# A decoder layer on one core: the second half of the input rows read in 32x32 blocks and turned on VectorE, the sample probabilities turned one step later

## The chip, the cores and the metric

The kernel runs on one core of a Trainium2 chip. A core has TensorE (PE, matrix products out of SBUF into PSUM), VectorE (DVE), ScalarE (ACT), GpSimd (POOL), and queues from which the engines and SyncE (SP) issue DMA transfers. The metric is the device time of one execution in microseconds (us), lower is better: 977.61 us before the change (median of 3 runs, 977.39 to 978.35).

## The reference

One layer of a hybrid decoder, over a prompt of 512 tokens and 32 sample tokens (8 sequences of 4), model width 1024, in float32. Cut to what matters here:

```python
h = x * rsqrt(mean(x * x, axis=-1) + EPS) * g          # RMSNorm of the rows
xr, q, k, v, g = split(h @ w_in)                       # one combined input projection, 4608 columns in 128-wide chunks
m = (sigmoid(g_A) * (lru(conv(xr)) @ w_lru_o) + sigmoid(g_B) * (attention(q, k, v) @ w_attn_o)) @ w_out
x = x + RMSNorm(m)
x = x + RMSNorm((gelu(gate) * val) @ w_down)           # gate, val: conv(RMSNorm(x) @ w_up)
```

The attention of the prompt looks back over 128 keys; that of the sample tokens over a cache of 128 keys and the new ones. Besides the rows, the kernel gives back the states of the recurrence, of the convolutions and the key and value caches.

## The kernel before

The activations lie turned: a tile holds 128 channels on its partitions and the 544 tokens along its columns, in two halves a = 0 (tokens 0 to 255) and a = 1 (tokens 256 to 543: 256 of the prompt and the 32 of the sample group). Every float32 operand of a product is split into a high and a low part, and three products stand for one: high by high, low by high, high by low.

**The input.** The rows of x arrive with tokens on the partitions (`xload`, L377), 128 tokens by 512 channels in each transfer. TensorE turns them through an identity matrix into PSUM: the first half in `turn_a` (L468), 16 transposes, and the second in `turn_b` (L523), 24 transposes: for each of 8 channel tiles k two blocks of 128 tokens and the 32 sample tokens. `hsplit` (L452) multiplies the turned tile by the norm's gain and splits it: ACT writes the high part hH[k], DVE the low part hL[k] = x*g - hH. The root of each row's mean square (`xsquare` for the sums, `roots` for the rest) is applied later, to the results of the projection: `roots` makes a diagonal tile dg on DVE, and a product ones by dg on TensorE (`ps_rep`) spreads it over the partitions as `rep`. The turned rows themselves are needed again for the residual some 320 us later: `keep_a` and `keep_b` copy them from PSUM into tiles xn, `put_away` (L515) sends these to DRAM from POOL's queue, and `x_again` (L1130) reads them back from SP's queue, 8 transfers.

**The projection.** `step` (L344) multiplies one 128-wide chunk of w_in by one half of h: 8 tiles by 3 products, 24 matmuls, into one of 3 PSUM buffers of the pool psm. After the matmuls `tick` runs what the other engines have to do at that place: the generators whose time has come (`sides`: a table of step numbers, `start_at`, says which of them starts at which step), the results of the step before (`late`), the splitting of the next weight chunk (`wsplit_hi` on ACT, L283, and `wsplit_lo` on DVE, L290), and the list `last`. So the order of the instructions on PE, ACT, DVE and POOL is that in which this code writes them, and each engine works its list off in order; SP's list follows from the same program.

The chunks come in the order 16, 18, 8, 9, 10, 11, 17, ... (16 and 17 are keys, 18 and 19 values, the others queries). The first `FIRST = 5` are multiplied by half 0 while half 1 is still being turned, then the same 5 by half 1, and from there every chunk by both halves. In the half-0 steps (`mmhalf_low_last`, L323) the products with the low weights come last; in the half-1 steps (`mmhalf`, L335) each tile k has its three products at once, so that hL[k] is needed right after hH[k]. `norms` (L560) is the generator around the change: it issues `keep_a`, the two calls of `turn_b`, the sums of squares of the rows 256 and up, and `roots(2, 5)`.

**Weights.** `wload` (L251) reads a chunk of 512 KB from SP's queue into one of 5 buffers raw. Chunks 16, 18, 8, 9 and 10 are asked for at the head of the program, chunk 11 as the sixth, after the many small loads of gains, biases and tables. Chunk 11 is split after the second half-1 step.

**Sample attention.** `sample_attn` (L873) runs twice (g = 0, 1) as a generator with a step of the projection between its parts: the probabilities are made by `softmax_b`, then turned on TensorE (`pst`, L909 to L911), copied, multiplied by the values (`pso`), and turned back (`psot`, L928).

Of the kernel before, what the change touches and what calls it, by code (L numbers as in the profile page):

```python
# [11 lines left out]
F32 = mybir.dt.float32  # L12
# [5 lines left out]
P = 128  # L18
# [26 lines left out]
T_BUFS = 10  # L45
RAW_BUFS = 5
SLOT = 568
CH = 4
CHAIN = 10
# [27 lines left out]
FILL = 1  # L77
TURNED = 8
GATES = (51, 53, 55, 57, 72, 73, 74, 75)
# [44 lines left out]
def hawk_step(ctx, tc, I, O):  # L124
# [21 lines left out]
    def T(name, dt=F32):  # L146
        return tp.tile([P, FLAT + 4], dt, tag="t", name=name)

# [99 lines left out]
    def wname(i):  # L248
        return "_".join(str(z) for z in order[i])

    def wload(i):  # L251
        key = order[i]
        raw = wraw[i] = rp.tile([P, KD, P], F32, tag="raw", name="raw_" + wname(i))
        if key[0] == "wg":
            for z, nme in enumerate(("lru_wr", "lru_wi")):
                nc.sync.dma_start(out=raw[:, 4 * z:4 * z + 4, :],
                                  in_=I[nme][0, 4 * key[1]:4 * key[1] + 4].rearrange("n c d -> c n d"))
        else:
            nc.sync.dma_start(out=raw, in_=wsrc(key))
# [11 lines left out]
    def wsplit_hi(un, eng=None):  # L271
        i, u = un // 2, un % 2
        hl = []
        for x in "hl":
            if order[i] in in_slots:
                t_ = S(f"w{x}{u}_{wname(i)}", F32R)[:, 0:512]
                t_ = t_.rearrange("p (k n) -> p k n", k=4)
            else:
                t_ = wp.tile([P, 4, P], F32R, tag="w", name=f"w{x}{u}_{wname(i)}")
            hl.append(t_)  # L280
        raw = wraw[i][:, 4 * u:4 * u + 4, :]
        if eng is None:
            act.activation(hl[0], raw, AF.Copy)  # L283
        else:
            eng.tensor_copy(hl[0], raw)
        wunits[un] = hl
        return raw, hl
# [86 lines left out]
    act.activation(warm, epst, AF.Sqrt)  # L374
    xt = {}

# [74 lines left out]

    def hsplit(k, a, ps):  # L452
        g = pv[:, G_PRE + k:G_PRE + k + 1]
        act.activation(h.get(k, a, 0), ps, AF.Copy, scale=g)
        stt(h.get(k, a, 1), ps, g, f32(h.get(k, a, 0)), ALU.mult, ALU.subtract)

# [46 lines left out]

    xn = [S(f"xn{k}") for k in range(KD)]
    xdram = drp.tile([KD, P, NT], F32, name="xdram")

    tb = []

    def keep_a(k):
        act.copy(xn[k][:, 0:256], turned_a(k))  # L510

    def keep_b(k, ps):
        (dve.tensor_copy if k % 4 > 1 else act.copy)(xn[k][:, 256:NT], ps[:, :288])

    def put_away():  # L515
        for k in range(KD):
            pool.dma_start(out=xdram[k], in_=xn[k][:, 0:NT])
            yield
# [3 lines left out]

    def turn_b(ks):  # L523
        tb.extend(PX(f"ps_tb{k}") for k in ks)
        for group in ((2, 3), (4,)):
            for k in ks:
                for i in group:
                    t0, n, _ = TOK[i]
                    pe.transpose(tb[k][:, t0 - 256:t0 - 256 + n], xtile(i, k), ident[:n, :n])
# [30 lines left out]
    def norms():  # L560
        xsquare(0, 1, True)
        yield from roots(0, 2)
        yield
        last.extend(lambda k=k: keep_a(k) for k in (0, 4, 1, 5, 2, 6))
        last.append(lambda: xsquares(2))
        yield
        turn_b(range(4))
        last.extend(lambda k=k: keep_a(k) for k in (3, 7))
        yield
        turn_b(range(4, KD))  # L570
        last.extend(lambda i=i: xsquares(i) for i in (3, 4))
        yield
        yield from roots(2, 5)
        dve.tensor_scalar(rq, ss[:, 1, 0:4], SCALE, None, ALU.mult)
# [302 lines left out]
    def sample_attn(g):  # L877
# [28 lines left out]
        softmax_b(s3, 1, *se)  # L906
        yield
        px = PX(f"pst{g}")
# [141 lines left out]
    start_at(1, norms())  # L1050
    start_at(13, put_away())
    start_at(1, attn_tables())
# [3 lines left out]
    for hp in range(4):  # L1056
        start_at((3, 5, 11, 18)[hp], once(load_rep, hp))
        start_at((4, 8, 15, 24)[hp], once(load_btab, hp))
    start_at(12, sample_tables())
# [22 lines left out]
    for z, c in enumerate(qkv_order[:FIRST]):  # L1082
        step(("in", c), h, 1, in_done(c), target=2 * FIRST + (0, 2, 4, 6, 6)[z])
    for c in qkv_order[FIRST:]:
# [45 lines left out]
    def x_again():  # L1130
        for k in range(KD):
            nc.sync.dma_start(out=x1[k][:, 0:NT], in_=xdram[k])
        yield
# [874 lines left out]
```

## Time and profile before

| what | value |
|---|---|
| runs before | 977.39, 977.61, 978.35 us |
| profiled execution | 977.74 us, of which the span of the profile is 976.0 us |
| PE busy | 967.6 us, 99% of the span |
| DVE, ACT, POOL busy | 758.6, 551.0, 168.8 us |
| DMA | 143.07 MB, 147 GB/s |

A row of the timeline gives the start in us from the span's start, the duration, the engine, the line, the operation, what is written and read, how many alike were put together (x4), and in brackets the idle time of the engine before it and what ended that. Instructions of one engine overlap a little, so that the step from one start to the next is shorter than a duration. SPq is the issue of a DMA from SP's queue. The clock granted to TensorE was 0.998 in this execution.

### The profile page before, as it was taken

To read this page: it belongs to the slowest core of one execution; us is meant where nothing else is said; L and a number is where in the kernel's file an instruction comes from. 1 tells how busy PE (TensorE), PEld (TensorE's weight loads), DVE (VectorE), ACT (ScalarE), POOL (GpSimd) and SP (SyncE) were. 2 spreads that over 40 slices of the span, in tenths; PEclk is the share of its full clock that TensorE was granted. 3 is DMA by queue.
4 is the path that set the end of the run, shared out by engine and by line. 5 is a ranking of instruction groups with operands and counts; after the bars stand their busy time and mean duration, and the time that the engine had idled before them with its cause. 6 is when DMAs were issued, how large, how long until landed. Compare 5 with 4: busy or idle time off the path is not lost.

```text
span 976.0 us, 20122 instructions
## 1 busy us (share of the span) xinstructions
PE 967.6 (99%) x7668; PEld 959.9 (98%) x7668; DVE 758.6 (78%) x1632; ACT 551.0 (56%) x1344; POOL 168.8 (17%) x288
## 2 busy tenths in 40 slices
PE   9999999999999999999999999999999999999997
PEld 8999999999999999999999999999999999999996
DVE  5777888857858555699967888787888888888875
ACT  6544443467476435556767665655555555556652
POOL 2152000003306331230011111101011101011024
PEclk9999999999999999999999999999999999999999
DMA  7875535632334547136157585858586766768612
GB/s 217 237 239 163 151 88 147 161 93 87 109 113 126 175 121 189 45 122 184 39 114 189 126 191 129 184 137 177 140 179 157 169 156 160 166 140 221 201 30 92
DMA packets 234204, 143.07 MB, mean 147 GB/s; under 512 B 25012, under 2 KB 218940, under 8 KB 234076
## 3 DMA queue, kind: packets, MB, share of 16 engines
q1 hardware_dynamic: 224300, 120.21, 43.9%
q0 software_dynamic: 9696, 19.42, 11.9%
q10 hardware_dynamic: 112, 2.17, 0.6%
q8 instruction: 60, 0.98, 0.4%
q14 instruction: 36, 0.29, 0.1%
HBM read 115.59 MB, written 15.17 MB: 134 GB/s over the span
## 4 chain that ended last, share of the span: by engine, by line
PE 97%; DVE 1%; ACT 1%; DMA 0%; issue 0%; SPq 0%; POOL 0%; ACTq 0%; POOLq 0%
PE pmin L165 20%; PE pmdn L165 19%; PE pux L1536 16%; PE puy L1536 8%; PE pq L1536 7%; PE pmout L165 5%; PE pmlo L165 5%; PE pmao L165 5%; PE puz L1536 4%; PE pg L165 1%; PE pvp L165 1%; PE psc L165 1%; PE ptok L165 1%; DMA pt<-pd 0%; PE ps_warm L165 0%; PE pm_first L165 0%
## 5 line engine op out<-in xcount | busy, mean ns | idle before, releaser
L165 PE MATMUL pmin<-hH,wh_in 128*128 128x256 f32 (+1 forms) x568 | 164.0, 291 | 0.0
L165 PE MATMUL pmin<-hL,wh_in 128*128 128x256 f32 (+1 forms) x568 | 162.5, 288 | 0.0
L165 PE MATMUL pmin<-hH,wl_in 128*128 128x256 f32 (+1 forms) x568 | 159.3, 288 | 0.0
L165 PE MATMUL pmdn<-fH,wh_dn 128*128 128x256 f32 (+1 forms) x448 | 129.3, 289 | 0.0
L165 PE MATMUL pmdn<-fH,wl_dn 128*128 128x256 f32 (+1 forms) x448 | 129.2, 288 | 0.0
L165 PE MATMUL pmdn<-fL,wh_dn 128*128 128x256 f32 (+1 forms) x448 | 129.0, 288 | 0.0
L165 PEld LDWEIGHTS pmin<-hH,wh_in 128*128 128x128 f32 x568 | 107.3, 189 | 1.2 <-issue 1.0
L165 PEld LDWEIGHTS pmin<-hL,wh_in 128*128 128x128 f32 x568 | 107.4, 189 | 0.1
L165 PEld LDWEIGHTS pmin<-hH,wl_in 128*128 128x128 f32 x568 | 104.8, 188 | 0.2 <-issue 0.2
L177 DVE SCALAR_TENSOR_TENSOR uc<-u,fv,uc 128x560 f32<-128x560 f32 x128 | 102.0, 797 | 1.7 <-ACT uc L1567 1.1
L165 PEld LDWEIGHTS pmdn<-fL,wh_dn 128*128 128x128 f32 x448 | 84.4, 188 | 0.0
L165 PEld LDWEIGHTS pmdn<-fH,wl_dn 128*128 128x128 f32 x448 | 84.4, 188 | 0.0
L165 PEld LDWEIGHTS pmdn<-fH,wh_dn 128*128 128x128 f32 x448 | 84.4, 188 | 0.0
L1664 ACT COPY u<-pux 128x272 f32<-128x272 f32 x52 | 20.1, 386 | 84.4 <-PE pux L1536 84.2
L168 DVE TENSOR_TENSOR u<-puy,u 128x240 f32<-128x240 f32 (+2 forms) x78 | 24.6, 343 | 48.8 <-PE puy L1536 32.2
L174 DVE TENSOR_TENSOR ft<-ft,pmdn 128x256 f32<-128x256 f32 (+1 forms) x104 | 45.0, 434 | 15.7 <-PE pmdn L165 15.7
L283 ACT ACTIVATE wh_in<-raw_in 128x512 fp32r<-128x512 f32 x70 | 42.2, 625 | 20.7 <-issue 11.0
L290 DVE TENSOR_TENSOR wl_in<-raw_in,wh_in 128x512 fp32r<-128x512 f32 x70 | 47.8, 694 | 1.0 <-ACT wh_in L283 1.0
L1567 ACT ACTIVATE uc<-u,fv 128x560 f32<-128x560 f32 x64 | 48.2, 755 | 0.0
L779 ACT ACTIVATE s<-s,st 128x256 f32<-128x256 f32 (+1 forms) x32 | 15.2, 475 | 53.8 <-DVE st L776 46.1
L168 DVE TENSOR_TENSOR wl_dn<-raw_dn,wh_dn 128x512 fp32r<-128x512 f32 x56 | 38.3, 685 | 3.8 <-ACT wh_dn L1485 3.8
L1474 POOL DMA_DIRECT2D raw_up_s<-raw_up_s x26 | 22.4, 861 | 95.8 <-DMA raw_up_s<-raw_up__11277 5.4
(761 smaller groups left out, 3388.5 us busy)
## 6 DMA issues: line engine op xcount, KB each, us to landing
raw_in<-in_w_in_dram SPq DMA_DIRECT2D x35, 512.0 KB
raw_dn<-in_w_down_dram SPq DMA_DIRECT2D x56, 256.0 KB
raw_up_s<-in_w_up_dram SPq DMA_DIRECT2D x25, 512.0 KB
raw_up_s<-raw_up_s POOLq DMA_DIRECT2D x26, 256.0 KB, 5.3
raw_ao<-in_w_attn_o_dram SPq DMA_DIRECT2D x8, 512.0 KB
raw_lo<-in_w_lru_o_dram SPq DMA_DIRECT2D x8, 512.0 KB
raw_out<-in_w_out_dram SPq DMA_DIRECT2D x8, 512.0 KB
pd<-pb SPq DMA_DIRECT2D x12, 256.0 KB
```

Of the source, the lines that this page charges most:

```text
L165: pe.matmul(out, l, r, start=start, stop=stop)
L168: dve.tensor_tensor(out=out, in0=a, in1=b, op=ALU.subtract)
L174: dve.tensor_tensor(out=out, in0=a, in1=b, op=ALU.add)
L177: dve.scalar_tensor_tensor(out=out, in0=a, scalar=s_, in1=b, op0=op0, op1=op1)
L283: act.activation(hl[0], raw, AF.Copy)
L290: (eng or dve).tensor_tensor(out=hl[1], in0=raw, in1=f32(hl[0]), op=ALU.subtract)
L779: act.activation(s3[:, j, :], s3[:, j, :], AF.Exp, bias=ng[:, j:j + 1], accum_out=sm[:, j:j + 1])
L1474: pool.dma_start(out=w["p4"], in_=w["p2"], accum_op=ALU.add)
L1536: pe.matmul(ps[:, :HN], w, x, start=start and k == 0 and i == 0, stop=stop and k == 3 and i == 2, skip_group_check=True)
L1567: act.activation(yt[j][:, 0:FLATU], u[:, 0:FLATU], AF.Copy, scale=fv[:, j:j + 1])
L1664: act.copy(e[nm_], z)
```

## The change

The rows 256 to 511 and the 32 sample rows are now read a second time, by SP, in pieces of 32 channels (128 bytes): `xblocks(yp)` fills one of four tiles xl with 4 transfers of 32 partitions by 16 pieces each, `xblocks_sample` a fifth. In these tiles each 32x32 block lies where VectorE's transpose, which turns 32x32 blocks in place, leaves the 128 channels of a tile on its partitions. `turn_b(yp)` is now 4 VectorE transposes of 128x128 elements, called four times, and `turn_sample` 4 of 128x64; they write into four tiles xb, each of two channel tiles k. The destination of the four calls interleaves the tokens: one transpose writes every eighth column. The rows are still loaded as before for the sums of squares, but later. `hsplit` of half 1 reads xb in two pieces, 256 prompt columns and 32 sample columns, on ACT and on DVE. The 8 copies `keep_b` go, since xb is already in SBUF; `keep_a` copies whole banks, 4 of 512 columns in place of 8 of 256. `put_away` sends xb and xn as 4 and 4 transfers, `x_again` reads them back as 24 transfers in place of 8.

Around it: `FIRST` goes from 5 to 6, so chunk 11 also has its half-0 step early; its weights are loaded among the first, into slots of their own (`RAWS`). Some starts of side work move by a step or more. In `sample_attn` a `yield 2` puts the transposes `pst` one step later.

```diff
-FIRST = 5
+FIRST = 6
-TURNED = 8
+TURNED = 9
...
     def wload(i):
         key = order[i]
+        if i == RAWS:
+            wraw[i] = [S(f"raw{u}_{wname(i)}")[:, 0:512].rearrange("p (k n) -> p k n", k=4) for u in range(2)]
+            for u in range(2):
+                nc.sync.dma_start(out=wraw[i][u], in_=wsrc(key)[:, 4 * u:4 * u + 4, :])
+            return
...
+    def xblocks(yp):
+        xl[yp] = S(f"xl{yp}")
+        src = xp[2 * P:4 * P, :].rearrange("(t w y) (k b f) -> b w t (y k) f", w=4, y=2, k=KD, b=4)
+        for b in range(4):
+            nc.sync.dma_start(out=xl[yp][32 * b:32 * b + 32, 0:512].rearrange("p (x f) -> p x f", f=32), in_=src[b, yp])
...
     wload(3)
+    xblocks(0)
+    xblocks(1)
+    wload(4)
+    xblocks_sample()
+    wload(5)
+    xblocks(2)
+    xblocks(3)
     for i in (2, 3, 4):
         xload(i)
-    wload(4)
...
-    def hsplit(k, a, ps):
+    def hsplit(k, a, src, z=0):
         g = pv[:, G_PRE + k:G_PRE + k + 1]
-        act.activation(h.get(k, a, 0), ps, AF.Copy, scale=g)
-        stt(h.get(k, a, 1), ps, g, f32(h.get(k, a, 0)), ALU.mult, ALU.subtract)
+        hi, lo = (h.get(k, a, j) for j in range(2))
+        spans = [((256 * z, 256 * z + 256), (0, 256)), ((512 + 32 * z, 544 + 32 * z), (256, 288))] if a else [((0, 256), (0, 256))]
+        for (i0, i1), (o0, o1) in spans:
+            act.activation(hi[:, o0:o1], src[:, i0:i1], AF.Copy, scale=g)
+        for (i0, i1), (o0, o1) in spans:
+            stt(lo[:, o0:o1], src[:, i0:i1], g, f32(hi[:, o0:o1]), ALU.mult, ALU.subtract)
...
-    def keep_a(k):
-        act.copy(xn[k][:, 0:256], turned_a(k))
-
-    def keep_b(k, ps):
-        (dve.tensor_copy if k % 4 > 1 else act.copy)(xn[k][:, 256:NT], ps[:, :288])
+    def keep_a(z):
+        act.copy(xn[z][:, 0:512], ps_ta[z])
...
-    def turn_b(ks):
-        tb.extend(PX(f"ps_tb{k}") for k in ks)
-        for group in ((2, 3), (4,)):
-            for k in ks:
-                for i in group:
-                    t0, n, _ = TOK[i]
-                    pe.transpose(tb[k][:, t0 - 256:t0 - 256 + n], xtile(i, k), ident[:n, :n])
-        for k in ks:
-            last.append(lambda k=k, ps=tb[k]: hsplit(k, 1, ps[:, :288]))
-        last.extend(lambda k=k, ps=tb[k]: keep_b(k, ps) for k in ks)
+    def turn_b(yp):
+        for kp in range(4):
+            if not yp:
+                xb[kp] = T(f"xb{kp}")
+            o = xb[kp][:, 0:512].rearrange("p (k t w y) -> p w y k t", k=2, w=4, y=2)[:, yp]
+            dve.transpose(o, xl[yp][:, 0:512].rearrange("p (y w k t) -> p w y k t", y=2, w=4, k=2)[:, kp])
+
+    def turn_sample():
+        for kp in range(4):
+            dve.transpose(xb[kp][:, 512:576], xl[4][:, 64 * kp:64 * kp + 64])
...
-        last.extend(lambda k=k: keep_a(k) for k in (0, 4, 1, 5, 2, 6))
-        last.append(lambda: xsquares(2))
-        yield
-        turn_b(range(4))
-        last.extend(lambda k=k: keep_a(k) for k in (3, 7))
-        yield
-        turn_b(range(4, KD))
-        last.extend(lambda i=i: xsquares(i) for i in (3, 4))
+        last.extend(lambda z=z: keep_a(z) for z in range(4))
+        yield
+        last.extend(lambda yp=yp: turn_b(yp) for yp in range(2))
+        yield
+        last.extend(lambda yp=yp: turn_b(yp) for yp in range(2, 4))
+        last.append(turn_sample)
+        last.extend(lambda k=k: split_b(k) for k in range(KD))
+        yield
+        last.extend(lambda i=i: xsquares(i) for i in (2, 3, 4))
...
         softmax_b(s3, 1, *se)
-        yield
+        yield 2
...
         for k in range(KD):
-            nc.sync.dma_start(out=x1[k][:, 0:NT], in_=xdram[k])
+            nc.sync.dma_start(out=x1[k][:, 0:256], in_=xdram[k % 4][:, k // 4 * 256:k // 4 * 256 + 256])
+            for lo, hi, z in ((256, SEQ, 256 * (k % 2)), (SEQ, NT, 512 + NS * (k % 2))):
+                nc.sync.dma_start(out=x1[k][:, lo:hi], in_=xdramb[k // 2][:, z:z + hi - lo])
```

On VectorE the change shows first between the half-0 steps and the first half-1 step. Before, there stand the split of chunk 10 (wl: low weights), the low part of query head 0 (qL), the first four low parts of half 1, and two of the copies that go (xn):

```order
L290 TENSOR_TENSOR wl0_in_10_449<-raw_in_10_136,wh0_in_10_448 128x512
L290 TENSOR_TENSOR wl1_in_10_452<-raw_in_10_136,wh1_in_10_451 128x512
L168 TENSOR_TENSOR qL0_475<-pmin_8_0_361,qH0_474 128x256
L177 SCALAR_TENSOR_TENSOR hL0_154<-ps_tb0_454,pv_141,hH0_153 128x288
L177 SCALAR_TENSOR_TENSOR hL1_156<-ps_tb1_455,pv_141,hH1_155 128x288
L177 SCALAR_TENSOR_TENSOR hL2_158<-ps_tb2_456,pv_141,hH2_157 128x288
L177 SCALAR_TENSOR_TENSOR hL3_160<-ps_tb3_457,pv_141,hH3_159 128x288
L513 COPY xn2_250<-ps_tb2_456 128x288
L513 COPY xn3_251<-ps_tb3_457 128x288
L168 TENSOR_TENSOR qL1_535<-pmin_9_0_421,qH1_534 128x256
```

Now, one step further on, behind the low part of query head 1, stand the second eight of the sixteen transposes, the four of the sample rows, and only behind all of them the low parts, in two pieces each:

```order
L170 TENSOR_TENSOR qL1_526<-pmin_9_0_438,qH1_525 128x256
L556 STREAM_TRANSPOSE xb0_477<-xl2_145 128x2x64
L556 STREAM_TRANSPOSE xb1_479<-xl2_145 128x2x64
...
L556 STREAM_TRANSPOSE xb0_477<-xl3_150 128x2x64
L556 STREAM_TRANSPOSE xb1_479<-xl3_150 128x2x64
...
L560 STREAM_TRANSPOSE xb0_477<-xl4_136 128x64
L560 STREAM_TRANSPOSE xb1_479<-xl4_136 128x64
...
L179 SCALAR_TENSOR_TENSOR hL0_183<-xb0_477,pv_170,hH0_182 128x256
L179 SCALAR_TENSOR_TENSOR hL0_183<-xb0_477,pv_170,hH0_182 128x32
L179 SCALAR_TENSOR_TENSOR hL1_185<-xb0_477,pv_170,hH1_184 128x256
```

What moved: the low parts of half 1, which stood in two groups behind two steps, stand in one group of 16 instructions behind 20 transposes.

On SP's queue, from the load of chunk 9 on, there stood the rows 256 and up (x2, x3) with the sample rows (x4), the weights of chunk 10, and then the small loads:

```order
L259 DMA raw_in_9_122<-in_w_in_dram 128x8x128
L381 DMA x2_0_124<-in_x_prompt_dram 128x512
L381 DMA x2_1_126<-in_x_prompt_dram 128x512
L381 DMA x3_0_128<-in_x_prompt_dram 128x512
L381 DMA x3_1_130<-in_x_prompt_dram 128x512
L381 DMA x4_0_132<-in_x_sample_dram 32x512
L381 DMA x4_1_134<-in_x_sample_dram 32x512
L259 DMA raw_in_10_136<-in_w_in_dram 128x8x128
L401 DMA rows_a_97<-in_norm_mix_post_dram 8x128
```

Now the pieces xl stand ahead of them, four transfers to a row, with chunks 10 and 11 between:

```order
L266 DMA raw_in_9_122<-in_w_in_dram 128x8x128
L388 DMA xl0_124<-in_x_prompt_dram 32x16x32 x4
L388 DMA xl1_129<-in_x_prompt_dram 32x16x32 x4
L266 DMA raw_in_10_134<-in_w_in_dram 128x8x128
L394 DMA xl4_136<-in_x_sample_dram 32x8x32 x4
L258 DMA raw0_in_11_141<-in_w_in_dram 128x4x128
L258 DMA raw1_in_11_142<-in_w_in_dram 128x4x128
L388 DMA xl2_145<-in_x_prompt_dram 32x16x32 x4
L388 DMA xl3_150<-in_x_prompt_dram 32x16x32 x4
L400 DMA x2_0_155<-in_x_prompt_dram 128x512
```

What moved: 22 more transfers stand ahead of the small loads, and so ahead of the next weight chunk behind these, which was chunk 11 and is now chunk 17.

More of the change, by code (lines that the diff above doesn't have):

```diff
@@ L46 @@
 RAW_BUFS = 5
+RAWS = 5
 SLOT = 568
+TSLOT = 576
 CH = 4
@@ L280, in wsplit_hi @@
             hl.append(t_)
-        raw = wraw[i][:, 4 * u:4 * u + 4, :]
+        raw = wraw[i][u] if i == RAWS else wraw[i][:, 4 * u:4 * u + 4, :]
         if eng is None:
@@ L374, in hawk_step, with xblocks_sample @@
     act.activation(warm, epst, AF.Sqrt)
-    xt = {}
+    xt, xl = {}, {}
+    def xblocks(yp):
[3 more added lines that the diff above has]
+            nc.sync.dma_start(out=xl[yp][32 * b:32 * b + 32, 0:512].rearrange("p (x f) -> p x f", f=32), in_=src[b, yp])
+    def xblocks_sample():
+        xl[4] = S("xl4")
+        src = xs.rearrange("t (k b f) -> b t k f", b=4, f=32)
+        for b in range(4):
+            nc.sync.dma_start(out=xl[4][32 * b:32 * b + 32, 0:256].rearrange("p (k f) -> p k f", f=32), in_=src[b])
     def xload(i, halves=(0, 1)):
@@ L502, in hawk_step @@
     xsquare(1, 1, False)
-    xn = [S(f"xn{k}") for k in range(KD)]
-    xdram = drp.tile([KD, P, NT], F32, name="xdram")
-    tb = []
-    def keep_a(k):
-        act.copy(xn[k][:, 0:256], turned_a(k))
-    def keep_b(k, ps):
-        (dve.tensor_copy if k % 4 > 1 else act.copy)(xn[k][:, 256:NT], ps[:, :288])
-    def put_away():
-        for k in range(KD):
-            pool.dma_start(out=xdram[k], in_=xn[k][:, 0:NT])
+    xn, xb = [S(f"xn{z}") for z in range(4)], {}
+    xdram = drp.tile([4, P, 512], F32, name="xdram")
+    xdramb = drp.tile([4, P, 576], F32, name="xdramb")
+    def keep_a(z):
+        act.copy(xn[z][:, 0:512], ps_ta[z])
+    def put_away():
+        for kp in range(4):
+            pool.dma_start(out=xdramb[kp], in_=xb[kp])
+        yield 4
+        for z in range(4):
+            pool.dma_start(out=xdram[z], in_=xn[z][:, 0:512])
             yield
@@ L1082, in hawk_step @@
     for z, c in enumerate(qkv_order[:FIRST]):
-        step(("in", c), h, 1, in_done(c), target=2 * FIRST + (0, 2, 4, 6, 6)[z])
+        step(("in", c), h, 1, in_done(c), target=2 * FIRST + (0, 2, 4, 6, 6, 6)[z])
     for c in qkv_order[FIRST:]:
```

11 lines of the change are left out of this document (7 added, 4 removed).

## Prediction

> **What bounds the kernel now.** I read the page first (busy time, the chain that ended last), then the waits of TensorE (PE), then the timeline of each engine over the stretch of the change, 19 to 42 us. From the page, the span, the busy times and the chain:
>
> ```profile
> span 976.0 us, 20122 instructions
> ...
> PE 967.6 (99%) x7668; PEld 959.9 (98%) x7668; DVE 758.6 (78%) x1632; ACT 551.0 (56%) x1344; POOL 168.8 (17%) x288
> ...
> PE 97%; DVE 1%; ACT 1%; DMA 0%; issue 0%; SPq 0%; POOL 0%; ACTq 0%; POOLq 0%
> ```
>
> PE is busy in 99% of the span and carries 97% of the chain. So work taken off PE shortens the time one for one, as long as no new wait comes in its place, and each us for which PE waits longer is a us more. The waits of PE hold one that the change is aimed at (columns: us, times, longest):
>
> ```profile
> PE pst L909 <- DVE ss L787: 0.7, 1, 0.7
> ```
>
> The timeline of PE around the change (start, duration; only the rows used are kept):
>
> ```profile
> 12.17 0.28 PE L165 MATMUL pmin<-hH,wh_in 128*128 128x256 f32 x1
> ...
> 15.03 0.28 PE L165 MATMUL pmin<-hH,wh_in 128*128 128x256 f32 x1
> ...
> 18.84 0.37 PE L165 MATMUL pmin<-hH,wh_in 128*128 128x256 f32 x1
> ...
> 21.78 1.40 PE L529 MATMUL ps_tb<-ident,x 128*128 128x128 f32 x12
> ...
> 23.11 0.38 PE L165 MATMUL pmin<-hH,wh_in 128*128 128x256 f32 x1
> ...
> 26.04 1.40 PE L529 MATMUL ps_tb<-ident,x 128*128 128x128 f32 x12
> ...
> 30.68 0.29 PE L165 MATMUL pmin<-hH,wh_in 128*128 128x288 f32 x1
> ...
> 33.97 0.72 PE L165 MATMUL ps_rep<-dg,ones 128*128 128x288 f32 x2
> 34.31 0.51 PE L165 MATMUL pmin<-hH,wh_in 128*128 128x288 f32 x1
> ...
> 37.72 0.22 PE L165 MATMUL psc<-kH,qH 128*128 128x128 f32 x1
> ...
> 38.34 0.35 PE L165 MATMUL pmin<-hH,wh_in 128*128 128x288 f32 x1
> ```
>
> Steps follow one another with no gap: a half-0 step from 12.17 to 15.03, the two groups of transposes at 21.78 and 26.04, half-1 steps up to 33.97, where `ps_rep` needs the diagonal tiles dg of the roots. PE does not wait there today, but VectorE (DVE) finishes just in time, as its rows below show.
>
> **The change part by part.** *Taken off PE.* A group of 12 transposes takes 23.11 − 21.78 = 1.33 us. The steps beside them are a little longer than a plain one: 23.11 to 26.04 is 2.93 and 18.84 to 21.78 is 2.94 against 2.86, so .08 for each break. Two groups give 2 × (1.33 + .08) = 2.82 us. `pst` moved a step later ends its wait, 0.67 us (0.7 in the row; it is put behind a whole step, many times that). Moving `pso` and `psot` along with it costs nothing, since later steps of the projection still lie between them and the projection that uses the result. Gain without new waits: 2.82 + .67 = 3.49 us.
>
> *The new DVE list.* The sixth half-0 step (chunk 11) only changes places with a later one: PE's total of steps is the same. So the old list's `ps_rep`, put behind one more half-0 step, would start at 33.97 + 2.86 = 36.83. That is the mark against which the new time of `ps_rep` counts; from there both lists go on alike. DVE's rows before, from the split of chunk 10 to the first use of `rep`, and two of its block transposes from the attention (stretch 47 to 54 us):
>
> ```profile
> 22.40 1.29 DVE L290 TENSOR_TENSOR wl_in<-raw_in,wh_in 128x512 fp32r<-128x512 f32 x2 [1.02 <-ACT wh_in L283]
> 23.61 0.42 DVE L168 TENSOR_TENSOR qL<-pmin,qH 128x256 fp32r<-128x256 f32 x1
> 23.94 1.78 DVE L177 SCALAR_TENSOR_TENSOR hL<-ps_tb,pv,hH 128x288 fp32r<-128x288 f32 x4
> 25.64 0.81 DVE L513 COPY xn<-ps_tb 128x288 f32<-128x288 f32 x2
> ...
> 30.26 0.68 DVE L437 SCALAR_TENSOR_TENSOR jk<-x 128x512 f32<-128x512 f32 x1
> ...
> 30.87 0.68 DVE L437 SCALAR_TENSOR_TENSOR jk<-x 32x512 f32<-32x512 f32 x1
> ...
> 31.48 0.41 DVE L168 TENSOR_TENSOR qL<-pmin,qH 128x256 fp32r<-128x256 f32 x1
> 31.82 0.14 DVE L174 TENSOR_TENSOR ss<-ss 128x3 f32<-128x3 f32 x1
> ...
> 33.73 0.17 DVE L574 TENSOR_SCALAR rq<-ss 128x4 f32<-128x4 f32 x1
> ...
> 35.16 0.46 DVE L171 TENSOR_TENSOR ks<-pmin,rep 128x288 f32<-128x288 f32 x1 [1.27 <-ACT rep L553]
> ```
>
> ```profile
> 47.55 0.43 DVE L821 STREAM_TRANSPOSE pb<-s 128x256 f32<-128x256 f32 x1
> 47.91 0.71 DVE L177 SCALAR_TENSOR_TENSOR s<-psc,rq,btab 128x512 f32<-128x512 f32 x1
> ...
> 53.41 0.70 DVE L821 STREAM_TRANSPOSE pb<-s 128x512 f32<-128x512 f32 x1
> 54.03 0.71 DVE L177 SCALAR_TENSOR_TENSOR s<-psc,rq,btab 128x512 f32<-128x512 f32 x1
> ```
>
> Prices, always from start to next start. A transpose takes .36 us for 256 columns and .62 for 512, so .26 for each 256 more; drawn down, .36 − .13 = .23 for 128 and .165 for 64. The four hL take (25.64 − 23.94)/4 = .425 for 288 columns; by the same slope .39 for 256 and .165 for 32, together .555 in place of .425. A jk is .61, a qL .33 (23.61 to 23.94), a wl pair 1.21 (22.40 to 23.61), and the chain of the roots from ss to rq 33.73 − 31.82 = 1.91. No row shows a transpose that writes every eighth column, nor one of 128 or 64 columns; .23 is the drawn-down price at the plain rate. The bounds are .13 (the columns alone) and .36 (the 256-column row, which a write at half rate would also give); I take .23, since the slope of two rows leads to it. An hL out of SBUF in place of PSUM may be shorter: the jk row, SBUF to SBUF, drawn down gives .61 − .27 = .34 for 256, so 8 × .05 = .4 us less at most; I stay with the same operation's row.
>
> ACT sets when DVE starts:
>
> ```profile
> 19.50 1.73 ACT L510 COPY xn<-ps_ta 128x256 f32<-128x256 f32 x6
> 21.69 1.19 ACT L283 ACTIVATE wh_in<-raw_in 128x512 fp32r<-128x512 f32 x2
> 22.73 0.42 ACT L708 ACTIVATE qH<-pmin 128x256 fp32r<-128x256 f32 x1
> 23.03 1.70 ACT L454 ACTIVATE hH<-ps_tb,pv 128x288 fp32r<-128x288 f32 x4
> ```
>
> In place of six copies of 256 columns and an unfinished rest stand four of 512 at the pace of the wh pair, (22.73 − 21.69)/2 = .52: 19.50 + 2.08 = 21.58, against 21.69. So chunk 10 is split as before, and DVE's first qL starts at 21.58 + (23.61 − 21.69) = 23.50. From there DVE is never without work:
>
> - qL .33, then eight transposes 8 × .23 = 1.84: 25.67
> - wl of chunk 11, 1.21: 26.88; qL .33: 27.21
> - eight transposes 1.84: 29.05; four for the sample 4 × .165 = .66: 29.71
> - sixteen hL pieces 8 × .555 = 4.44: 34.15 (ACT needs less for the high parts: 1.70/4 = .43 for 288 in one piece, and it starts earlier)
> - qL .33, three jk 3 × .61 = 1.83, qL .33: 36.64
> - roots to rq 1.91: 38.55; `ps_rep` follows rq by 33.97 − 33.73 = .24: **38.79**
>
> The mark was 36.83, so `ps_rep` starts 1.96 us later. PE's own work does not hide this: PE waits some .4 us for the split of chunk 10, then about 3 us spread over the first half-1 step for the hL, and about 1 us for dg. The waits eat the 2.82 us and 1.96 more. The hiding cover of before was that the low parts of half 1 came in two groups of four, each behind a step of PE.
>
> *Queues.* SP, ACT's waits for the next chunk, and the read-back some 300 us later:
>
> ```profile
> 27.43 16.09 SPq L259 DMA_DIRECT2D raw_in<-in_w_in_dram  x8
> ```
>
> ```profile
> 32.56 1.15 ACT L283 ACTIVATE wh_in<-raw_in 128x512 fp32r<-128x512 f32 x2 [0.21 <-DMA raw_in<-in_w_in_dram]
> ...
> 34.73 0.40 ACT L553 COPY rep<-ps_rep 128x288 f32<-128x288 f32 x1 [1.01 <-PE ps_rep L165]
> ```
>
> ```profile
> 325.38 4.63 SPq L1132 DMA_DIRECT2D x<-xdram  x8
> ```
>
> ```profile
> L283 ACT ACTIVATE wh_out<-raw_out x16: 615/622/632, 355.4 to 385.2; 128x512 fp32r<-128x512 f32 x16
> ```
>
> Chunk 11, issued at 27.43 before, was waited for until 32.56: 5.13 us at most. Chunk 17 now stands in that place, behind 22 transfers more. At the pace of the read-back, 4.63/8 = .58 each, this is at most 12.8 us later, an issue at 40.2 and a landing at 45.4; at least it is no later, with a landing by 32.6, if the gaps that the queue's small loads leave today take them all up. I estimate an issue at 36.9, nearer the upper end because chunk 11 was already waited for today, and so a landing at 42.0. ACT then splits it (22.73 − 21.69 = 1.04), copies rep (35.16 − 34.73 = .43), and DVE frees the first PSUM buffer with ks (.46): 43.9. PE asks for that buffer behind ps_rep, the products of psc and one step: 38.79 + .34 + (38.34 − 37.72) + (37.72 − 34.31) = 43.2, with a small group of transposes (.3) at 43.5. By these numbers PE waits .4 us, by the bounds of the landing 0 to 3.8; as the roots may hold PE up anyway by as much, I take .2. The 16 more read-backs at .58 take 9.3 us, to about 339; the weights behind them are first split at 355.4, so this is hidden, and uncovered it would be 9.3 us.
>
> *Sum.* +1.96 (ps_rep) − .67 (pst) + .2 (chunk 17) = +1.5 us. The profiled execution took 977.74 us, its span 976.0; that is .13 above the median of the three runs. 977.61 + 1.5 = **979.1 us**.
>
> **The rivals.** *A, the strided write is slow (slower).* Each of the sixteen transposes writes columns 32 bytes apart. If that costs as much again as the columns (.13), DVE ends 16 × .13 = 2.1 us later, and PE with it: 979.1 + 2.1 = 981.2. It decides from .26 us for a transpose, where .47 us on sixteen brings the total past 979.57, the 0.2% bound. For it: the destination is the only one of its kind here. Against it: the source and number of elements are plain. [...]
>
> *B, DVE is quicker than drawn (faster).* If the small pieces cost .1 in place of .165, the transposes .15 and the hL .34, DVE ends 12 × .065 + 16 × .08 + 8 × .05 = 2.5 us earlier, at 36.3, and PE is back in front: it gains most of the 3.49, some 974.1 to 976.5. For it: instructions that overlap on DVE. Against it: all prices already are start to start.
>
> *C, the queue decides.* If chunk 17 lands 2 us later still, at 44, its .2 becomes 2.2: 981.1; from a landing of 42.3 or so the total passes 979.57. For it: 22 transfers, many of 128-byte pieces, go ahead of it. Against it: the small loads behind idle the queue today.
>
> **How the numbers follow.** Measurement tells about 0.2% from no change, 2 us: faster is under 975.65, slower over 979.57. The forecast has .52 (own range 977.6 to 980.0, .10 of it over 979.57), A .26, C .07, B .15. Faster is B, .15; slower is A, C and the .10, .43; the rest, .42, is the same. The range of 975.5 to 982.0 takes in A and C with the bounds of the transposes, and the upper end of B; about 2 in 10 is left out.
>
> **What would show it.** In the profile after: no ps_tb rows; no wait of pst; the xb transposes at .23 us from start to start (over .26: A; under .16: B); the last hL at about 34, ps_rep at about 38.8 (36.8 or earlier: B); a wait of PE for hL of some 3 us in all and one for dg of about 1; ACT's wait for raw 17 ending near 42 (44: C). It is wrong if PE's waits between 22 and 44 us add up to less than 2.5 us or more than 6.5.

## The result, and the profile after

The changed kernel takes 987.93 us (median of 5 runs, 986.69 to 989.44) where the kernel before takes 977.61: a ratio of 1.0105 (95% interval 1.009 to 1.012). It is slower by some 10 us. The forecast was 979.1 with a range up to 982.0. The profiled execution took 987.5 us, with a span of 985.4 against 976.0 before.

The page of the changed kernel, span, busy times and chain:

```profile
span 985.4 us, 20154 instructions
...
PE 967.8 (98%) x7644; PEld 958.7 (97%) x7644; DVE 762.9 (77%) x1656; ACT 550.8 (56%) x1344; POOL 168.4 (17%) x288
...
PE 82%; DVE 7%; DMA 3%; SPq 3%; ACT 3%; issue 1%; POOL 1%; DVEq 0%; ACTq 0%; POOLq 0%
```

PE has 24 instructions fewer and is as long busy as before, but carries 82% of the chain in place of 97%: transfers, SP's queue and VectorE have taken the rest. Its waits name the places (us, times, longest):

```profile
PE pmin L167 <- ACT hH L482: 4.6, 1, 4.6
PE pmin L167 <- DVE ks L173: 3.3, 1, 3.3
...
PE pmin L167 <- ACT wh_in L290: 0.9, 1, 0.9
```

`pst` is gone from the list, and two large waits are new. The timeline of PE shows where they lie, and the one of VectorE what stood behind them:

```profile
27.34 1.10 PE L167 MATMUL pmin<-hH,wl_in 128*128 128x256 f32 x8
33.04 0.61 PE L167 MATMUL pmin<-hH,wh_in 128*128 128x288 f32 x1 [4.60 <-ACT hH L482]
...
42.22 0.75 PE L167 MATMUL ps_rep<-dg,ones 128*128 128x288 f32 x2
...
50.44 0.40 PE L167 MATMUL pmin<-hH,wh_in 128*128 128x288 f32 x1 [3.31 <-DVE ks L173]
```

```profile
24.00 2.24 DVE L556 STREAM_TRANSPOSE xb<-xl 128x128 f32<-128x128 f32 x8
...
28.55 1.09 DVE L556 STREAM_TRANSPOSE xb<-xl 128x128 f32<-128x128 f32 x4 [0.86 <-DMA xl<-in_x_prompt_dram]
31.48 1.10 DVE L556 STREAM_TRANSPOSE xb<-xl 128x128 f32<-128x128 f32 x4 [1.84 <-DMA xl<-in_x_prompt_dram]
...
49.92 0.46 DVE L173 TENSOR_TENSOR ks<-pmin,rep 128x288 f32<-128x288 f32 x1 [7.69 <-ACT rep L584]
```

The first wait is that for the pieces xl2 and xl3: VectorE stands idle before both, and PE, which has finished its six half-0 steps at about 28.4, waits for the first high part. Behind the second stands ACT, which has the split of chunk 17 ahead of the copy of rep, and behind that SP, which asks for chunk 17 at 44.59 in place of the 27.43 at which the old list asked for its next chunk:

```profile
48.46 1.15 ACT L290 ACTIVATE wh_in<-raw_in 128x512 fp32r<-128x512 f32 x2 [7.76 <-DMA raw_in<-in_w_in_dram]
49.51 0.38 ACT L584 COPY rep<-ps_rep 128x288 f32<-128x288 f32 x1
```

```profile
9.67 7.46 SPq L388 DMA_DIRECT2D xl<-in_x_prompt_dram  x8
...
17.71 2.68 SPq L394 DMA_DIRECT2D xl<-in_x_sample_dram  x4
20.44 1.15 SPq L258 DMA_DIRECT2D raw_in<-in_w_in_dram  x2
21.63 6.67 SPq L388 DMA_DIRECT2D xl<-in_x_prompt_dram  x8
...
31.48 0.43 SPq L426 DMA_DIRECT2D rows_a<-in_norm_mix_post_dram  x1
...
44.59 15.10 SPq L266 DMA_DIRECT2D raw_in<-in_w_in_dram  x8
```

The 22 transfers that now stand ahead of the small loads hold SP for 7.46 + 2.68 + 1.15 + 6.67 = 17.96 us, .82 each, and that is the whole delay of 17.16. The small loads make up nothing of it: from the first of them to the weight chunk SP takes 44.59 − 31.48 = 13.11 us now and took 27.43 − 14.74 = 12.69 before.

```profile
14.74 0.33 SPq L401 DMA_DIRECT2D rows_a<-in_norm_mix_post_dram  x1
```

The chain of waits over 20 to 52 us (start, duration, what) tells the same in order: the issues of the pieces (L388) one after the other, the row loads (L400), then two transfers on whose landing a later small load waits, then chunk 17, its split, rep, ks. The 7.01 and 5.23 are the times of those transfers and not waits of SP, which issues other loads meanwhile; from 28 to 44.6 us it stands still for some 4 us in all.

```profile
...
29.82 7.01 DMA x<-in_x_prompt_dram
...
37.99 5.23 DMA rows_f<-in_ffn_conv_w_dram
...
44.59 3.78 DMA raw_in<-in_w_in_dram
...
48.46 1.15 ACT wh_in L290 x2
49.60 0.30 ACT rep L584
```

A ledger by PE's own marks. The mark for `ps_rep` was 36.83; it starts at 42.22, **+5.39 us**. From there to the sample biases (`ps_bs`) the kernel before takes 59.07 − 33.97 = 25.10, less the step of 2.86 that now lies ahead, 22.24; the changed one takes 68.16 − 42.22 = 25.94, **+3.70**, of which 3.31 is the wait for ks. That makes 9.09 of the 9.4 us between the spans.

```profile
59.07 0.70 PE L165 MATMUL ps_bs<-ohs,lt 128*128 128x320 f32 x2
```

```profile
68.16 0.81 PE L167 MATMUL ps_bs<-ohs,lt 128*128 128x320 f32 x2
```

### The profile page after: what moved, and what is told of

Same layout as the page of the kernel before. It is cut to its first block, busy times and chain, and to the rows that moved or that the text cites. A ratio compares the mean times of both kernels' runs of the same rounds, so it can differ in the third digit from the quotient of the medians.

```text
span 985.4 us, 20154 instructions
## 1 busy us (share of the span) xinstructions
PE 967.8 (98%) x7644; PEld 958.7 (97%) x7644; DVE 762.9 (77%) x1656; ACT 550.8 (56%) x1344; POOL 168.4 (17%) x288
## 4 chain that ended last, share of the span: by engine, by line
PE 82%; DVE 7%; DMA 3%; SPq 3%; ACT 3%; issue 1%; POOL 1%; DVEq 0%; ACTq 0%; POOLq 0%
PE pmdn L167 17%; PE pux L1570 16%; PE pmin L167 12%; PE puy L1570 8%; PE pq L1570 6%; PE pmout L167 5%; PE pmao L167 5%; PE pmlo L167 5%; PE puz L1570 4%; SPq L388 1%; PE pg L167 1%; DMA raw_in<-in_w_in_dram 1%; PE ptok L167 1%; DMA x<-in_x_prompt_dram 1%; ACT s L811 1%
```

## The experiments

**Theory.** The re-reading of a megabyte in 128-byte pieces is what costs: it makes its own last pieces late, and chunk 17 behind them. **Rivals.** The engines' new lists cost the time whatever the loads; the half clock of TensorE, which the records of the changed kernel show at 0.50 from 31.6 to 38.5 us, costs it; or only the place in SP's list is wrong. All times stand beside runs of the kernel before on the same chip (977.6 to 978.0).

**e2_rows: the pieces left out.**

```diff
-    xblocks(0)
-    xblocks(1)
-    wload(4)
-    xblocks_sample()
-    wload(5)
-    xblocks(2)
-    xblocks(3)
     for i in (2, 3, 4):
         xload(i)
+    wload(4)
+    wload(5)
+    for yp in range(4):
+        xl[yp] = xt[2 + yp // 2, yp % 2]
+    xl[4] = xt[2, 0]
```

> The changed kernel without the 20 loads of 128-byte pieces: the 20 transposes take the row tiles of the rows 256 and up, which are loaded where they were before the change; so every instruction of the engines stays, and the values of half 1 are wrong. Theory (the loads cost the time, by both waits): PE waits neither 4.6 us for hH nor 3.3 for ks; what is left is VectorE's list with transposes of .26 us, about 2 us behind the mark as forecast, so 979 to 980.5. Rival (the engines' new lists cost the time, whatever the loads): over 985.

Measured: 980.51 us, ratio 1.0028 (1.0017 to 1.0039). 7.4 of the 10 us are gone, and of the lists only SP's has changed: the pieces are out of it, and the rows stand ahead of chunk 10 again. VectorE's timeline has no idle time left from its first transpose to the roots, and PE waits for it:

```profile
23.66 2.24 DVE L554 STREAM_TRANSPOSE xb<-x 128x128 f32<-128x128 f32 x8
25.73 1.28 DVE L297 TENSOR_TENSOR wl_in<-raw_in,wh_in 128x512 fp32r<-128x512 f32 x2
26.92 0.42 DVE L170 TENSOR_TENSOR qL<-pmin,qH 128x256 fp32r<-128x256 f32 x1
27.26 2.06 DVE L554 STREAM_TRANSPOSE xb<-x 128x128 f32<-128x128 f32 x8
29.18 0.55 DVE L558 STREAM_TRANSPOSE xb<-x 128x64 f32<-128x64 f32 x4
29.66 4.83 DVE L179 SCALAR_TENSOR_TENSOR hL<-xb,pv,hH 128x256 fp32r<-128x256 f32 x16
34.40 0.42 DVE L170 TENSOR_TENSOR qL<-pmin,qH 128x256 fp32r<-128x256 f32 x1
```

```profile
38.97 0.75 PE L167 MATMUL ps_rep<-dg,ones 128*128 128x288 f32 x2 [0.63 <-DVE dg L572]
```

`ps_rep` starts at 38.97, where the forecast had 38.79. This kernel is the world that the forecast worked out, and it costs 2.7 us where the forecast had 1.5: VectorE's list is behind the mark by 2.1 us, and the 0.67 of `pst` were not gained (e5_pst); some .3 us of the difference are not accounted for. So of the 5.39 us, 2.14 are VectorE's list and 3.25 the loads: .86 and 1.84 us in which VectorE waits for xl2 and xl3, .34 by which its first transpose is later (24.00 against 23.66; ACT waited .59 us for chunk 10), and .2 spread.

**e12_loads: the pieces alone, in the kernel before.**

```diff
     wload(4)
+    src = xp[2 * P:4 * P, :].rearrange("(t w y) (k b f) -> b w t (y k) f", w=4, y=2, k=KD, b=4)
+    for yp in range(4):
+        spare = S(f"xl{yp}")
+        for b in range(4):
+            nc.sync.dma_start(out=spare[32 * b:32 * b + 32, 0:512].rearrange("p (x f) -> p x f", f=32), in_=src[b, yp])
```

> The kernel before the change with one part of it alone: the 16 loads of 128-byte pieces (a megabyte, into four tiles that nothing reads), behind the load of chunk 10 and ahead of the small loads; every engine's list stays as it was. Theory (the loads cost by themselves, through the chunk behind them): at the .65 to .93 us that each took, chunk 11 is asked for 10 to 14 us later than 27.43, ACT waits for it until 43 to 46 with the copy of rep behind it, PE runs out of PSUM buffers at about 42 and waits 3 to 5 us for ks: 980.5 to 983. Rival (transfers fit into gaps that the small loads leave, and only the new lists of the engines hurt): within 1 us of 977.6.

Measured: 986.24 us, ratio 1.0081 (1.0064 to 1.0098): the loads cost 8 us in a kernel that does nothing with them. The mechanism is as expected, the price higher. Chunk 11 is asked for at 37.55, ACT waits until 41.41, PE for 4.9 us:

```profile
41.41 1.15 ACT L283 ACTIVATE wh_in<-raw_in 128x512 fp32r<-128x512 f32 x2 [9.24 <-DMA raw_in<-in_w_in_dram]
```

```profile
43.39 0.61 PE L165 MATMUL pmin<-hH,wh_in 128*128 128x288 f32 x1 [4.91 <-DVE ks L171]
```

The rest, which the expectation had not counted, is the clock: behind the wait the granted clock is 0.50, as the stretches of 4 us show in their third last column, and the step from 43.39 takes until 49.15, 5.8 us in place of 3.2. The wait and this stretch are 4.9 + 2.6 = 7.5 of the 8.2 us.

```profile
44.00:48.00 4.00, 4.00 (x18) 4.00 (x18) 3.46 (x8) 2.81 (x8) 0.00 (x0) 0.50 1.21 291
```

**e4_fill: does the half clock cost anything in the changed kernel?**

```diff
+NDUM = 18
...
+            if key == order[FIRST - 1]:
+                pf = PX("ps_fill")
+                for z in range(NDUM):
+                    mm(pf[:, (z % 4) * P:(z % 4 + 1) * P], ones, ones, True, True)
```

> The changed kernel with 18 idle products of ones by ones on PE behind the sixth half-0 step, in the 4.6 us in which it waits for hH, so that its granted clock may stay at 1.0 (it fell to 0.5 for 6.8 us). Theory (the half clock costs nearly nothing, since VectorE's hL come at .60 us a tile and the roots at 42.07 set ps_rep): the first half-1 step runs faster, ps_rep still starts at about 42.2, the time stays within 0.6 us of 987.9. Rival (the half clock costs what it stretches, 5.5 us for a step in place of 3.2): 985.6 or less.

Measured: 988.65 us, ratio 1.0111 (1.0096 to 1.0126), 0.7 above the changed kernel and so a little outside the 0.6 named, but on the other side from the rival. PE's wait for hH is down from 4.6 to 0.5 us, the clock stays at 1.00 from 28 to 44 us, and `ps_rep` starts at 42.64. So the half clock from 31.6 us on does not delay `ps_rep`, and is no cause of the 10 us in the changed kernel: while it lasted, VectorE's list was the longer one, with the root rq only at 42.07. In e4_fill the products are slower later, behind its wait of 3.77 us for ks: .24 us from start to start until 54.58, .13 from there; the two runs don't tell what that cost.

```profile
42.07 0.16 DVE L606 TENSOR_SCALAR rq<-ss 128x4 f32<-128x4 f32 x1
```

**e3_wide and e11_half: the shape and the number of the pieces.** e3_wide:

```diff
-            nc.sync.dma_start(out=xl[yp][32 * b:32 * b + 32, 0:512].rearrange("p (x f) -> p x f", f=32), in_=src[b, yp])
+            r = 2 * P + 64 * yp + 32 * (b // 2)
+            nc.sync.dma_start(out=xl[yp][32 * b:32 * b + 32, 0:512], in_=xp[r:r + 32, 512 * (b % 2):512 * (b % 2) + 512])
```

> The changed kernel with as many transfers of as many bytes for the pieces xl, in the same places of SP's list, but each partition's 2 KB in one run in place of 16 pieces of 128 bytes; the values of half 1 are wrong. Theory A (the small pieces make the transfers slow: 128 bytes take 13 ns on a DMA engine where 512 take 27): xl3 lands 2 us or more earlier, PE's wait of 4.6 falls below 3, the time to 985.5 or less. Theory B (their number and place in SP's list make them late): xl3 lands within 0.7 us of 31.4 and the time stays within 1 us of 987.9.

Measured: 984.84 us, ratio 1.0077 (1.0062 to 1.0092). Theory A: the transposes of xl2 and xl3 start at 27.48 with 0.37 us of idle time before them, and PE waits 2.1 us for hH, hardly more than the 1.7 of e2_rows. The same bytes in runs of 2 KB are there in time. But chunk 17 is still late:

```profile
PE pmin L167 <- DVE ks L173: 3.0, 1, 3.0
PE pmin L167 <- ACT hH L483: 2.1, 1, 2.1
```

e11_half, half as many pieces:

```diff
-    xblocks(2)
-    xblocks(3)
+    xl[2], xl[3] = xl[0], xl[1]
```

> The changed kernel with half of the pieces: xl2 and xl3 are not loaded, their transposes take xl0 and xl1 (values of half 1 partly wrong). Theory (the DMA engines' time is what the pieces cost, wherever in the list): half of the 7.4 us between the changed kernel and e2_rows comes back or more, 981 to 984.3, and PE's wait for hH is 1.7 to 2.2 as in e2_rows, since nothing late stands before the transposes any more. Rival (the cost lies in the first pieces, which hold up chunks 10 and 11): over 985.

Measured: 982.73 us, ratio 1.0052 (1.0038 to 1.0065). 5.2 of the 7.4 us come back, as the theory had it: the wait for hH is 1.7 as in e2_rows, and that for ks 1.5.

**e1_raw17: chunk 17 asked for earlier.**

```diff
+    wload(6)
     rows_b = rows_a[32:96, :]
```

> The changed kernel with one edit: the load of chunk 17 is asked for ahead of most of the small loads of gains, biases and tables. Theory (chunk 17 late: ACT has its split ahead of the copy of rep, so DVE's ks and with it a PSUM buffer wait for a weight that stands behind 20 small pieces): its load is issued some 6 us earlier, about 38.5 in place of 44.59, lands by about 43, ACT no longer waits 7.8 us, the 3.3 us of PE behind ks go, and the time falls by 3.3 us to about 984.6. Rival (VectorE's list alone sets the time, as the forecast had it): the wait moves to the roots and the time stays at 987.9, within 0.7.

Measured: 985.97 us, ratio 1.0085 (1.007 to 1.010): 2 us less, not 3.3, and the runs of the two kernels overlap a little (985.02 to 987.25 here, 986.69 to 989.44 there). The load is issued at 38.73 as expected, but it takes 5.4 us to land in place of 3.8, and the next chunk is now late as well, which ACT shows:

```profile
44.17 1.15 ACT L290 ACTIVATE wh_in<-raw_in 128x512 fp32r<-128x512 f32 x2 [4.88 <-DMA raw_in<-in_w_in_dram]
...
48.83 1.15 ACT L290 ACTIVATE wh_in<-raw_in 128x512 fp32r<-128x512 f32 x2 [1.94 <-DMA raw_in<-in_w_in_dram]
```

PE's wait for ks falls to 0.4, and 1.6 us of waits for qL appear further on; in the profiled execution, the fastest of the four, part of the gain is that VectorE's wait for xl3 ended 1.4 us earlier, although nothing ahead of it had changed. So the place of chunk 17 is a part of the cause, and moving it moves the shortage on to the chunks behind.

**e9_wide17: both.** e3_wide with the line of e1_raw17.

> e3_wide (as many bytes for xl, in runs of 2 KB, values of half 1 wrong) with the load of chunk 17 asked for early as in e1_raw17. Theory (the 128-byte pieces and the place of chunk 17 make up nearly all that the loads cost): the 3.0 us of PE behind ks go as well, 981.8 within 0.7, near the 980.5 of e2_rows. Rival (the megabyte read twice is short of bandwidth in any shape, so a later chunk comes late instead): 983 or more.

Measured: 983.15 us, ratio 1.0054 (1.0039 to 1.0069), just on the rival's side: the wait for ks falls from 3.0 to 0.7, and waits of 1.8 for qL come instead. In both shapes in which it was read the second megabyte leaves later chunks late; the shape is worth about 3 of the 7.4 us.

**e6_pool: another queue.**

```diff
...
-    xblocks(2)
-    xblocks(3)
...
+    xblocks(2, pool)
+    xblocks(3, pool)
...
+    wload(6)
     rows_b = rows_a[32:96, :]
```

> The changed kernel with the load of chunk 17 asked for early as in e1_raw17, and with 8 of the 16 loads of 128-byte pieces (xl2, xl3) issued from GpSimd's queue from about 12 us on, while it idles, instead of SP's. Theory (SP's list is what makes both late: each piece waits its turn behind the weights): xl2 and xl3 land before 27 us, SP reaches chunk 17 about 6 us sooner, both waits of PE shrink to those of e2_rows, 980.5 within 0.8. Rival (the DMA engines, not the queue, are what is short): xl3 still lands after 29, the time stays above 983.

Measured: 986.21 us, ratio 1.0085 (1.0071 to 1.0099). The rival, with a turn that it had not named: xl2 and xl3 are in time, but now chunk 10 is late, and PE waits for that as long as it had waited for hH:

```profile
PE pmin L167 <- ACT wh_in L290: 4.4, 1, 4.4
```

Chunk 10 is asked for .8 us earlier than in the changed kernel (16.41 against 17.18), and ACT can start on it 3.6 us later (25.38 against 21.80). So not SP's queue is what is short. The stretch from 9 to 32 us in the view of the transfers (busy tenths of the DMA engines in 40 slices, GB/s, packets), first before, then after, then e6_pool:

```profile
DMA  9999999999999999720010311678942000369999
...
DMA packets 6617, 4.57 MB, mean 199 GB/s; under 512 B 923, under 2 KB 5875, under 8 KB 6615
```

```profile
DMA  9999999999897255689994499956969958498997
...
DMA packets 14427, 4.46 MB, mean 194 GB/s; under 512 B 9763, under 2 KB 14122, under 8 KB 14425
```

```profile
DMA  9999999999999999999999999649588798799984
...
DMA packets 10813, 4.93 MB, mean 214 GB/s; under 512 B 5727, under 2 KB 10087, under 8 KB 10811
```

Before, the DMA engines fall idle in the middle of the stretch. After, they are busy nearly throughout, and yet by 32 us they have moved no more bytes (4.46 against 4.57 MB), in twice as many packets. From the records of single packets in the changed kernel's trace, the same stretch: 9216 packets of 128 bytes took 14.7 ns on average, those of 512 bytes 31.9, so 8.7 against 16.1 bytes a ns on an engine.

**e7_merge and e8_squares: a shorter list for VectorE.** e7_merge is e6_pool with

```diff
-        src = xp[2 * P:4 * P, :].rearrange("(t w y) (k b f) -> b w t (y k) f", w=4, y=2, k=KD, b=4)
+        src = xp[2 * P:4 * P, :].rearrange("(w t y) (k b f) -> b w t (y k) f", w=4, y=2, k=KD, b=4)
...
-        spans = [((256 * z, 256 * z + 256), (0, 256)), ((512 + 32 * z, 544 + 32 * z), (256, 288))] if a else [((0, 256), (0, 256))]
+        spans = [((288 * z, 288 * z + 288), (0, 288))] if a else [((0, 256), (0, 256))]
```

and the destinations of the transposes and the read-backs set to match, and e8_squares is e7_merge with

```diff
+        last.extend(lambda z=z: xsquare(2, z, True) for z in range(2))
+        last.extend(lambda z=z: xsquare(3, z, True) for z in range(2))
         last.extend(lambda yp=yp: turn_b(yp) for yp in range(2, 4))
...
-        last.extend(lambda i=i: xsquares(i) for i in (2, 3, 4))
+        last.append(lambda: xsquares(4))
```

> e6_pool with VectorE's list made shorter: prompt and sample tokens of a channel tile lie side by side in xb, so that half 1 is split in one piece of 288 columns on ACT and on DVE in place of 256 and 32 (8 instructions fewer on each); and a transpose writes every second column in place of every eighth, with rows paired (w t y) in place of (t w y). Theory (once the loads are there, VectorE's list sets ps_rep, as the forecast had it): the eight hL take .43 a tile in place of .60, 1.4 us less, and ps_rep comes about 1.4 us earlier than in e6_pool, 979 or less; transposes at .23 in place of .26 if the stride costs, which would be .5 us more. Rival (something else still holds ps_rep): no more than 0.3 us against e6_pool.

> e7_merge with the sums of squares of rows 256 to 511 all on ACT, ahead of its high parts, where it idled 4 to 6 us; VectorE keeps one of the three. Theory: VectorE's list is 1.2 us shorter, the roots no longer set ps_rep but PE's own steps do; up to 1.2 us under e7_merge, 977 to 978.3. Rival (the squares wait for rows that land after 28 us and hold up the high parts behind them on ACT): slower than e7_merge by 0.5 us or more.

Measured: 986.57 us, ratio 1.0089 (1.0075 to 1.0102), and 985.88 us, ratio 1.0079 (1.0064 to 1.0094). Both theories miss by 7 us or more: neither run differs from e6_pool's 986.21 by more than the runs scatter. In e7_merge `ps_rep` does start 1.7 us earlier (41.32 against 42.97), the shorter list is real. At `ps_bs` 1.0 us of it is left (65.3 against 66.3), with .3 more of waits for qL (1.4 against 1.1), and in e8_squares nothing (66.4). So beside the loads these two runs show no gain from a shorter list; where the rest of it went is not shown. The transposes that write every second column are cheaper:

```profile
27.86 1.65 DVE L557 STREAM_TRANSPOSE xb<-xl 128x128 f32<-128x128 f32 x8
29.43 1.25 DVE L297 TENSOR_TENSOR wl_in<-raw_in,wh_in 128x512 fp32r<-128x512 f32 x2
```

(29.43 − 27.86)/8 = .196 us each, against (25.73 − 23.66)/8 = .259 for the first eight of e2_rows, with every eighth, and (29.18 − 27.26)/8 = .24 for its second eight.

**e10_free: the shorter list without the pieces.** The edits of e7_merge and e8_squares to the lists, put on e2_rows.

> e2_rows (no loads of pieces, transposes from the row tiles, values of half 1 wrong) with the shorter list of VectorE of e7_merge and e8_squares (half 1 split in pieces of 288, transposes that write every second column, two of the three sums of squares on ACT). Theory (with the loads out of the way VectorE's list alone is what is left of the loss, as the forecast's term had it): VectorE has 3.5 us less, the roots no longer set ps_rep, which starts at about 37, the total 977.6 to 979, no better than before the change. Rival (the 2.8 us taken off PE show at last): 975.5 or less.

Measured: 979.37 us, ratio 1.0017 (1.0008 to 1.0026), just above the theory's range and far from the rival's. VectorE's list is no longer the bound: `ps_rep` starts at 36.25, ahead of the mark.

```profile
36.25 0.65 PE L167 MATMUL ps_rep<-dg,ones 128*128 128x288 f32 x2
...
56.35 0.40 PE L167 MATMUL pmin<-hH,wh_in 128*128 128x288 f32 x1 [0.90 <-DVE qL L170]
```

It is 1.1 us better than e2_rows and still behind the kernel before; a wait of .9 us at 56.35 comes in its place. ACT waits 3.5 us for chunk 17 and 2.4 for the next in this run, which makes late chunks the likely reason; that was not tried. So even without its extra loads and with a shorter list, the change brought no gain.

**e5_pst: the sample probabilities alone.**

```diff
         softmax_b(s3, 1, *se)
-        yield
+        yield 2
```

> The kernel before the change with one edit, the sample probabilities turned a step later. Theory (the forecast's term): PE's wait of 0.67 us at the turn goes and nothing takes its place, 0.7 us faster, 976.9 where the kernel before has 977.6. Rival (the next sample group's scores then wait about 0.3 to 0.5 for the key cache on DVE, as in the changed kernel): only 0.2 to 0.4 us are left.

Measured: 977.73 us against 977.75, ratio 0.9999 (0.999 to 1.0008). The wait at `pst` is gone, but there is no gain to be seen: with it the scores of the second sample group have moved up on PE, from 177.9 to 176.2 us, and they now wait for the turned keys, for which VectorE had time before.

```profile
176.17 1.22 PE L165 MATMUL pss<-kcT,qs 128*32 128x256 f32 x8 [0.30 <-DVE kcT L891]
```

Of the versions tried, none beats the kernel before.

## Why the prediction was wrong, point by point

- **PE's gain of 2.82 us**: PE lost its 24 transposes, as said, and waited in their place; no run shows the gain paid out in full, and so none measures it.
- **VectorE's list**: right. Without the loads of pieces `ps_rep` came at 38.97, forecast 38.79. That it fits within .2 us is in part luck: the transposes took .259 and .24 in place of .23 and a pair of hL pieces 4.74/8 = .59 in place of .555, but the sample transposes .12 in place of .165, and the list started .17 us earlier than forecast (23.66 against 23.83).
- **"From there DVE is never without work"**: this is the step that failed. The sum let the transposes start as soon as VectorE came to them and never asked when xl2 and xl3 land. They stood behind 8 pieces, the sample pieces and two chunks on SP, and VectorE waited .86 and 1.84 us for them; with the later chunk 10, `ps_rep` came 3.25 us later than by the list alone.
- **The landing of chunk 17**: the mechanism was there (rival C), the size was not. The forecast took .58 us at most for a transfer, an issue at 36.9 and 40.2 at the latest. The 22 transfers took .82 on average, the pieces 7.46/8 = .93 and 6.67/8 = .83, so the .58 that was to be the most was too small; the small loads behind them took up nothing of it, and the issue was at 44.59, 4.4 us behind the latest that the forecast allowed. The term of .2 us became 3.3 to 3.7. Rival C's price of 2.2 was too small as well, and it had 7 in 100.
- **`pst`, −.67 us**: wrong. The wait went, and another of .30 with a slow start behind it came; the run of that edit alone shows no gain.
- **Rival A, the strided write**: the measured .24 to .26 us lie at and below the point from which it was to decide, and far from its .36. Against .196 with a stride of two columns (e7_merge) they are a quarter to a third longer, and the sixteen cost some .9 us more: real, and small beside the loads.
- **The read-backs and `keep_a`**: no wait showed at either; hidden, as said.
- **The sign that was to warn**: PE's waits between 22 and 44 us add up to .9 + 4.6 = 5.5, within the 2.5 to 6.5 that the forecast allowed. The sum fits by luck: besides chunk 10 PE waited once, for the first high part, and not spread over the step and for dg, and the second large wait lay behind 44.
- **The width of the range**: it had no term for the landing of the pieces and took every landing from rows of large transfers. The rows that the forecast used hold no price of a small piece, but the trace of the kernel before has 14464 packets of 128 bytes, which took 12.9 ns on average against 29.5 for those of 512. An estimate from that: the 8192 packets of the megabyte are 8192 × 12.9/16 = 6.6 us of all 16 DMA engines.

## What to carry to other kernels

Work was taken off the busiest engine here and paid with a second reading of its input, and that reading alone cost 8.2 us (e12_loads). So count the transfers ahead of every weight in the same list, price small pieces by packets and not by bytes (here 14.7 ns for 128 bytes against 31.9 for 512), and ask of each new tile when it lands before asking what the engine needs for it. A late load also cost what stood behind it: ACT, with the split of a chunk ahead of the copy of rep in its list, waited 7.76 us for chunk 17 and copied rep at 49.51, though `ps_rep` had started at 42.22. When a wait is removed by moving a step, look at what moves up behind it: its operand may have had exactly that time, as in e5_pst, where a wait of .30 us came in place of that of .67.

## What the runs showed of the hardware

- Packets of 128 bytes took 14.7 ns and packets of 512 bytes 31.9 in the changed kernel between 9 and 32 us: 8.7 against 16.1 bytes a ns, about half the rate. Over its whole execution packets of 128, 512 and 1024 bytes took 13.6, 29.5 and 51.6 ns: 9.4, 17.3 and 19.8 bytes a ns. With half of the pieces issued from POOL's queue (e6_pool), chunk 10 was asked for .8 us earlier than in the changed kernel, and ACT could start on it 3.6 us later.
- In the changed kernel the granted clock fell to 0.50 at 31.64, 3.2 us after PE's wait of 4.6 us began, and stayed there for 6.8 us. Behind the wait products of 288 columns stood .24 us from start to start for 5.4 us and .13 from there; in e12_loads, behind a wait of 4.9 us, .24 for 5.5 us and .13 from there. The length of the wait alone does not set this: in e7_merge, behind a wait of 4.6 us, products of 256 columns stood .21 us apart for 3.5 us only, and .12 from there. The slow products cost 2.6 us in e12_loads, where PE set the pace, and nothing that could be seen in the changed kernel, where VectorE's list did (`ps_rep` at 42.22, and at 42.64 in e4_fill with the clock at 1.00 from 28 to 44 us).
- A VectorE transpose of 128x128 took .24 to .26 us from start to start when it wrote every eighth column (e2_rows) and .196 with every second (e7_merge).
